# Carried transposes of a head pair, held back in the next pair's list of steps

## The chip, the cores and the metric

The kernel runs on one core of a Trainium2 chip. The metric is device microseconds (us) of one execution; less is better. The engines are called PE (TensorE), DVE (VectorE), ACT (ScalarE), POOL (GpSimd) and SP (SyncE, which issues most loads).

## The reference, cut to what matters

One inference step of a two-layer encoder trunk, in float32, over 1024 new frames of one stream (prompt) and 16 frames of each of 8 running streams (sample, with caches of 1024 past positions). Width 1024, heads of 64, MLP of 4096.

```python
# layer 0: 8 heads of stick-breaking attention beside a convolution branch
z = einsum('bqhd,bkhd->bhqk', q, k) * HEAD_DIM ** -0.5
log_keep = where(k_pos < q_pos, log_sigmoid(-z), 0)
between = cumsum(log_keep, axis=3, reverse=True) - log_keep
w = where(k_pos < q_pos, exp(log_sigmoid(z) + between), 0)
a_out = einsum('bhqk,bkhd->bqhd', w, v)
c_out = silu(layernorm(depthwise_conv31(a * sigmoid(g))))
x = x + concatenate([a_out, c_out]) @ w_out
# layer 1: 16 heads of softmax attention in a band of 9 chunks of 64
s = einsum('bqhd,bkhd->bhqk', q, k) * HEAD_DIM ** -0.5 + rel_bias
p = softmax(where(band, s, -inf))
x = x + (p @ v) @ w_out
# each layer: RMSNorm ahead of the mixer and of a squared-ReLU MLP, residuals; RMSNorm at the end
```

The outputs are the frames of prompt and sample, and the new caches.

## The kernel before

**Tiles and stages.** All 1152 frames are processed together, 128 on the partitions of a tile. A float32 matmul is done as three products of a hi and a lo part (`split`, L185 and L186: ACT copies the hi part, DVE subtracts to the lo part). Projections run in groups of 12 matmuls of 128x384: 8 chunks of 128 inputs by three products are 24, in two steps of 12. The order of the stages is mixer 0, MLP 0, mixer 1, MLP 1, last norm.

**Pairs.** Attention goes by pairs of heads: four pairs p in layer 0, eight in layer 1. A pair has eight jobs (2 heads i by 4 blocks t of 256 queries). A job is: scores for its two sub-blocks of 128 queries (`one`: matmuls `z` at L924 and L925 in layer 0, `zc` at L1201 and L1202 in layer 1), element-wise work on DVE and ACT, transposes of the weights through PE (`turn`: tiles `tpa` from L388 in layer 0, `tpc` from L455 in layer 1), their copies out of PSUM by ACT and DVE (`wa`; `whc` and `wlc`), and products with the values (`prod`: `ava` L398, `avc` L467, joined on DVE in `cpa`, `cpc`). In layer 0 the element-wise work is two ACT activations (`sg`, `kp`), a scan over `kp` on DVE (L907) and a product on DVE (L909), which leaves the weights in `sg`. In layer 1 it is a fused bias and maximum on DVE (L1165), an exponential on ACT (L1168), and a reciprocal and a scale on DVE (L1169, L1170), which leaves the weights in `s`. Names carry pair, head and block: `sg017` is pair 0, head 1, sub-block 7; `tpa0130` is pair 0, head 1, block t=3, group 0.

**What runs beside a pair.** The sample attention of the pair (`zs`, `zn`: scores against cached keys, which are loaded as tiles `ct..k`), the projection of the next pair (`proj`, PSUM tiles `psp` in layer 0 and `psc` in layer 1; in layer 0 also `ag`), and in layer 0 the 31 taps of the depthwise convolution on DVE (L735). In pair 3 of layer 0 the place of the projection is taken by the output projection `psoa`, whose input `cat` is loaded back from HBM (`cr`, L1062) and split.

**What sets the order.** All instructions of an engine run in the order in which the program records them, and that order comes from lists of `Step`s: a step has an estimated PE time `pe` (ns), a function that records its instructions, and, if wanted, a name, the name of a step that it comes `after`, and a `lag` in ns after that step's end. `merge` (L53) interleaves lists: it keeps a model clock `now`, and takes among the heads of all lists the one that is ready first, and among equal ones that whose list is least far along. A list is never reordered in itself, so a head that is not ready holds back all of its list. The first transposes of a job have `after` = the name of the job's last scores, with a lag of 4500 ns (L421, L491).

**Carried steps.** The last job of a pair (head 1, block 3) is not finished in the pair's own list: its transposes and products are `carry`, the first steps of the next pair's list (L985, L1238). There the name they come after is not among the names of the call: `merge` finds no end for it.

```python
steps = carry + [jobs[0][0]] + [Step(327.0, lambda p=p, g=g: expand_v(p, g)) for g in range(NG)]
...
run(level(merge(steps, sample, fill, mix), now))
```

Of the kernel before, what the change touches and what calls it, by code (L numbers as in the profile page):

```python
# [52 lines left out]
def merge(*lists):  # L53


    lists = [steps for steps in lists if steps]
    total = [sum(s.pe for s in steps) or 1.0 for steps in lists]
    at, done = [0] * len(lists), [0.0] * len(lists)
    out, now = [], 0.0
    ends = {s.name: 1e9 for steps in lists for s in steps if s.name}  # L60
    while True:
        heads = []
        for n, steps in enumerate(lists):
            if at[n] < len(steps):
                s = steps[at[n]]
                ready = max(now, ends.get(s.after, -1e9) + s.lag)
                heads.append((ready, (done[n] + 0.5 * s.pe) / total[n], n, s))
        if not heads:
            return out
        now, _, n, s = min(heads, key=lambda e: e[:3])  # L70
        out.append(s)
        at[n] += 1
        done[n] += s.pe
        now += s.pe
        if s.name:
            ends[s.name] = now
# [48 lines left out]
def tile_trunk(ctx, tc, ins, outs):  # L125
# [529 lines left out]
    def mixer0():  # L655
        with ExitStack() as st:
# [309 lines left out]
            for p in range(4):  # L966
# [29 lines left out]
                load = sample_caches(0, p, cp)  # L996
                sample = two_samples(*(sample_steps(0, p, bg, S, wk, load, soft, cs) for bg in range(2)))
                run(level(merge(steps, sample, fill, mix), now))
            return cat_t

# [96 lines left out]
    def mixer1(nx, win):  # L1097
        h, rstd = nx.h, nx.r
        with ExitStack() as st:
# [129 lines left out]
            for p in range(8):  # L1229
# [10 lines left out]
                if p == 7:  # L1240
                    bias_p(p, 0)
                    expand_qk(p)
                    run(merge(steps, ready_chunks(1, range(3), pp, cat_t)))
                    steps = []
# [13 lines left out]
                if p < 7:  # L1258
                    bias_p(p, 0)
                    if p:  # L1260
                        expand_qk(p)
                run(merge(steps, sample, fill, back))
            return cat_t

# [702 lines left out]
```

## Time and profile before

| What | Value |
|---|---|
| Median of 3 runs | 2751.92 us (2749.0 to 2752.41) |
| The profiled execution | 2750.03 us, its span 2748.2 us |
[...]
| PE busy | 2669.0 us (97%) |
| DVE busy | 2090.5 us (76%) |
| ACT busy | 1389.0 us (51%) |
| POOL busy | 328.3 us (12%) |

How to read it: the profile is of one execution, and its own time differs from the median by 1.9 us. The shares are means over stages with different limits. A row of a timeline gives the start and the length of one instruction, or of several alike in a row (x and their count), and in square brackets how long the engine was idle before it and what ended that. A row of windows gives a stretch and, for each engine, its busy time in it with the count of instructions.

### The profile page before, as it was taken

The page shows a single profiled execution, that of the slowest core. Times are in us where ns is not written, and L with a number is a line of the kernel's source. Part 1 is how long each engine was busy: PE and PEld are TensorE (multiplying, and loading weights), DVE is VectorE, ACT ScalarE, POOL GpSimd, SP SyncE. Part 2 cuts the span into 40 slices and gives each one's busy share as a digit, 9 for nine tenths or more (in the row PEclk, how much of TensorE's full clock was granted, in tenths as well). Part 3 has the DMA queues.
Part 4 walks back from the last instruction along what each step waited for, and adds up shares of the span by engine and source line. Part 5 has one row for each costly group of instructions (what it writes and reads, how often), then busy time and mean ns, then how long its engine had stood idle before and what let it go on. Part 6 is the DMA issues. An engine that isn't in the chain of part 4 may idle for free.

```text
span 2748.2 us, 50583 instructions
## 1 busy us (share of the span) xinstructions
PE 2669.0 (97%) x19362; PEld 2557.1 (93%) x19362; DVE 2090.5 (76%) x4117; ACT 1389.0 (51%) x2906; POOL 328.3 (12%) x599
## 2 busy tenths in 40 slices
PE   8999898999999999999999999998999999999998
PEld 8987776799999999999999999997999999999998
DVE  8999998888777755758577777778787777647577
ACT  5344456755554543435355555556555555434344
POOL 1100101041111100000011111110221111100001
PEclk9999999999999999999999999999999999999999
DMA  4434446454343377435444444446533343684344
GB/s 157 121 111 147 118 141 223 145 176 143 139 146 141 138 260 250 124 100 170 146 140 138 140 135 135 139 132 229 179 132 137 141 145 138 230 270 134 96 125 145
DMA packets 173203, 422.90 MB, mean 154 GB/s; under 512 B 25968, under 2 KB 53808, under 8 KB 170912
## 3 DMA queue, kind: packets, MB, share of 16 engines
q1 hardware_dynamic: 135696, 288.38, 33.1%
q0 software_dynamic: 37120, 131.27, 13.9%
q8 instruction: 152, 2.49, 0.4%
q14 instruction: 91, 0.75, 0.1%
q10 hardware_dynamic: 144, 0.02, 0.0%
HBM read 289.60 MB, written 117.34 MB: 148 GB/s over the span
## 4 chain that ended last, share of the span: by engine, by line
PE 76%; DVE 12%; ACT 4%; issue 4%; DMA 3%; POOL 0%; SPq 0%; DVEq 0%; ACTq 0%; POOLq 0%
PE um L1461 25%; PE pd L1686 25%; PE psc L225 10%; PE psp L225 3%; DVE y L735 3%; PE avc L467 2%; PE tpc L455 2%; DVE kp L907 2%; PE f L225 1%; PE psoa L225 1%; DMA cr<-cat_d 1%; PE zc L1201 1%; PE zc L1202 1%; PE zs L568 1%; PE so L602 1%
## 5 line engine op out<-in xcount | busy, mean ns | idle before, releaser
L225 PE MATMUL psc<-h,hl_wc 128*128 128x384 f32 x1728 | 327.2, 339 | 0.0
L225 PEld LDWEIGHTS psc<-h,hl_wc 128*128 128x128 f32 x1728 | 296.8, 188 | 13.3 <-issue 10.9
L1461 PE MATMUL um<-sl,hl_m 128*128 128x288 f32 x1548 | 240.3, 295 | 0.0
L1461 PEld LDWEIGHTS um<-sl,hl_m 128*128 128x128 f32 x1548 | 217.7, 188 | 0.0
L1686 PE MATMUL pd<-tm,hl_wd 128*128 128x288 f32 x1584 | 214.7, 294 | 0.0
L1686 PEld LDWEIGHTS pd<-tm,hl_wd 128*128 128x128 f32 x1584 | 211.3, 189 | 0.0
L735 DVE SCALAR_TENSOR_TENSOR y<-u,dw,y 128x1024 f32<-128x1024 f32 (+1 forms) x232 | 177.8, 806 | 0.6
L225 PE MATMUL psp<-h,hl_wi 128*128 128x384 f32 x864 | 165.7, 344 | 0.0
L1468 ACT ACTIVATE hdm<-hdm 128x288 f32<-128x288 f32 x192 | 84.7, 442 | 156.5 <-DVE hdm L1467 154.8
L225 PEld LDWEIGHTS psp<-h,hl_wi 128*128 128x128 f32 x864 | 150.9, 191 | 7.0 <-issue 6.2
L186 DVE TENSOR_TENSOR tm<-xr,tm 128x576 fp32r<-128x576 f32 (+1 forms) x120 | 85.8, 715 | 93.9 <-ACT tm L185 93.6
L185 ACT ACTIVATE tm<-xr 128x576 fp32r<-128x576 f32 (+1 forms) x120 | 77.6, 646 | 95.8 <-PE pd L1686 74.0
L1168 ACT ACTIVATE s<-s,mxc 128x640 f32<-128x640 f32 (+4 forms) x128 | 88.9, 694 | 60.2 <-DVE mxc L1165 58.6
L1461 PE MATMUL um<-sl,hl 128*128 128x288 f32 x756 | 119.1, 296 | 0.0
L1686 PE MATMUL pd<-th,hl_wd 128*128 128x288 f32 x792 | 113.7, 297 | 3.8 <-DVE th L186 3.7
L1686 PEld LDWEIGHTS pd<-th,hl_wd 128*128 128x128 f32 x792 | 108.2, 190 | 4.8 <-DVE th L186 4.2
L1686 PE MATMUL pd<-xr,hl_wd 128*128 128x288 f32 x792 | 112.4, 296 | 0.0
L1686 PEld LDWEIGHTS pd<-xr,hl_wd 128*128 128x128 f32 x792 | 108.0, 190 | 0.0
L1461 PEld LDWEIGHTS um<-sl,hl 128*128 128x128 f32 x756 | 106.4, 188 | 0.8
L1686 PE MATMUL pd<-tm,hl 128*128 128x288 f32 x768 | 104.9, 295 | 0.0
L1686 PEld LDWEIGHTS pd<-tm,hl 128*128 128x128 f32 x768 | 103.1, 188 | 0.0
L185 ACT ACTIVATE whc<-tpc 128x512 fp32r<-128x512 f32 (+1 forms) x144 | 72.5, 523 | 46.7 <-PE tpc L455 45.8
(526 smaller groups left out, 6637.0 us busy)
## 6 DMA issues: line engine op xcount, KB each, us to landing
xr<-hb_d SPq DMA_DIRECT2D x208, 288.0 KB, 3.0
xr<-in_w_up_dram SPq DMA_DIRECT2D x64, 512.0 KB, 4.2
hb_d<-hdm POOLq DMA_DIRECT2D x96, 288.0 KB, 2.4
hb_d<-t POOLq DMA_DIRECT2D x96, 288.0 KB, 2.4
wm<-in_w_down_dram SPq DMA_DIRECT2D x64, 256.0 KB, 4.0
st_wd<-in_w_down_dram SPq DMA_DIRECT2D x64, 256.0 KB, 3.5
st_wc<-in_w_in_c_dram SPq DMA_DIRECT2D x44, 256.0 KB, 2.9
xm_d<-xo POOLq DMA_DIRECT2D x16, 576.0 KB, 3.5
```

The lines of the kernel that those rows point to most:

```text
L185: ACT(hi, src, AF.Copy)
L186: return tt(lo, src, f(hi), ALU.subtract)
L225: mm(ps()[:, :G], hl[:, a, at:at + P], act[g][k // 4][b][:, k % 4, :], start=n == 0, stop=n == len(todo) - 1)
L455: nc.tensor.transpose(tp[:, c0 + q * P:c0 + (q + 1) * P], blocks.get(j, tile_q), ident)
L467: mm(st["av"][:, o0:o0 + n], vs[:, j, i].rearrange("p a d -> p (a d)"), src[:, c0:c0 + n], start=st["done"] == 0, stop=st["done"] == nmm - 1)
L568: mm(box["z"][at // 512][own, at % 512:at % 512 + kw], qb[:, own], k[:, b * kw:b * kw + kw], start=True, stop=True)
L735: stt(src if j == CW - 1 else dst, src, wj, dst, ALU.mult, ALU.add)
L907: nc.vector.tensor_tensor_scan(keep[:, 0:n][:, ::-1], keep[:, 0:n][:, ::-1], ones[:, 0:1].to_broadcast([P, n]), 1.0, ALU.mult, ALU.mult)
L1168: ACT(s[:, :n], s[:, :n], AF.Exp, bias=mx, scale=-1.0, accum_out=tot)
L1461: mm(banks[b, n][:, :TQ], w[:, a, c * P:c * P + P], combo(key, c)[:, h, n * TQ:n * TQ + TQ], start=k < 3 and c == 0 and i == 0, stop=c == ...
L1468: ACT(y, y, AF.Relu)
L1686: mm(ps, w[:, a, m * P:m * P + P], b[:, h, (n - ns[0]) * TQ:(n - ns[0]) * TQ + TQ], start=first and s == 0, stop=j == NJ - 1 and s == 2, s ...
```

## The change

In `merge`, a head whose `after` names a step that is not in this call had been ready at once (its end taken as minus 1e9 ns). Now the end of such a step is taken as 2000 ns before the start of the list, so that a carried `turn` step with its lag of 4500 ns is ready at 2500 ns of the model clock. Steps without an `after` are treated as before. A blank line is added above, so that every line number behind it is one higher in the changed kernel.

```diff
             if at[n] < len(steps):
                 s = steps[at[n]]
-                ready = max(now, ends.get(s.after, -1e9) + s.lag)
+
+                ready = max(now, ends.get(s.after, -2000.0 if s.after else -1e9) + s.lag)
                 heads.append((ready, (done[n] + 0.5 * s.pe) / total[n], n, s))
```

The order of all five engines differs from boundary 0 to 1 of layer 0 up to that layer's last pair, and from boundary 0 to 1 of layer 1 up to 5 to 6; the last pair of layer 1 and the MLPs stand as before. No instruction is added or left out.

PE at boundary 0 to 1 of layer 0, before (`psp200` is the first projection group of pair 2; `h0` its inputs, `hl_wi` its weights):

```order
L398 MATMUL ava012_2221<-wa0122_2179,vs0_747 64x128
L388 MATMUL tpa0130_2261<-ident_69,sg016_2058 128x128
L225 MATMUL psp200_2268<-h0_00_159,hl_wi12_0_2037 128x384
...
L225 MATMUL psp200_2268<-h0_11_164,hl_wi12_0_2037 128x384
L388 MATMUL tpa0130_2261<-ident_69,sg017_2125 128x128
...
L225 MATMUL psp200_2268<-h0_30_171,hl_wi12_0_2037 128x384
L388 MATMUL tpa0131_2284<-ident_69,sg016_2058 128x128
...
L568 MATMUL zs0100_2298<-ct01k00_2300,qb0_124 32x256 x4
```

and with the change:

```order
L399 MATMUL ava012_2221<-wa0122_2179,vs0_747 64x128
L226 MATMUL psp200_2261<-h0_00_159,hl_wi12_0_2037 128x384
...
L226 MATMUL psp200_2261<-h0_70_190,hl_wi12_1_2042 128x384
L389 MATMUL tpa0130_2291<-ident_69,sg016_2058 128x128
L389 MATMUL tpa0130_2291<-ident_69,sg017_2125 128x128
...
L569 MATMUL zs0100_2307<-ct01k00_2309,qb0_124 32x256 x4
```

Before, five matmuls of the group stand between the first transpose and the first that reads `sg017`; now all 24 stand ahead of both.

PE at the tail of pair 1 of layer 1, before (`zc116` are the scores of sub-block 6, `tpc1120` and `tpc1121` transpose `s114` and `s115`, `sq111` is a transpose of the sample part):

```order
L467 MATMUL avc111_16154<-wlc1111_16122,vs1_14196 128x128
L1202 MATMUL zc116384_16172<-l1_14195,q1_14191 128x256
L225 MATMUL psc222_16141<-h1_40_13712,hl_wc8_1_15619 128x384
...
L225 MATMUL psc222_16141<-h1_70_13826,hl_wc8_1_15619 128x384
L455 MATMUL tpc1120_16195<-ident_69,s114_16093 128x128
L455 MATMUL tpc1120_16195<-ident_69,s115_16125 128x128
...
L610 MATMUL sq111_16213<-ident_69,sb111_16081 128x128
L467 MATMUL avc112_16220<-whc1120_16200,vs1_14196 128x256 x2
```

and with the change:

```order
L1203 MATMUL zc115384_16143<-l1_14195,q1_14191 128x256
L226 MATMUL psc222_16084<-h1_40_13712,hl_wc8_1_15619 128x384
...
L226 MATMUL psc222_16084<-h1_70_13826,hl_wc8_1_15619 128x384
L468 MATMUL avc111_16166<-whc1110_16127,vs1_14196 128x256 x2
...
L1203 MATMUL zc116384_16184<-l1_14195,q1_14191 128x256
L611 MATMUL sq111_16195<-ident_69,sb111_16081 128x128
L456 MATMUL tpc1120_16202<-ident_69,s114_16107 128x128
...
L456 MATMUL tpc1120_16202<-ident_69,s115_16139 128x128
L456 MATMUL tpc1121_16211<-ident_69,s115_16139 128x128
```

The second half of `psc222`, which stood directly ahead of the transposes, now stands one place earlier, ahead of the products `avc111`. Ahead of these, between `zc115` and `avc111`, the first half of `psc222` stood before.

DVE at the same place, before (`sv12` takes `psc222` out of PSUM, `hl_wc10` is a weight split):

```order
L1170 TENSOR_SCALAR s114_16093<-s114_16093,totc114_16104 128x640
L186 TENSOR_TENSOR hl_wc10_0_16288<-st_wc10_0_16286,hl_wc10_0_16288 128x512
L1169 RECIPROCAL totc115_16136<-totc115_16136 128x1
L1165 ISA s116_16168,mxc1160_16175<-zc1160_16169,bp11_15729 128x384
L1170 TENSOR_SCALAR s115_16125<-s115_16125,totc115_16136 128x640
L477 TENSOR_TENSOR cpc111_16165<-avc111_16154,atc111_16163 64x256
```

and with the change:

```order
L1171 TENSOR_SCALAR s114_16107<-s114_16107,totc114_16118 128x640
L1123 TENSOR_TENSOR sv12_15999<-psc222_16084,rh1_14160 128x384
L187 TENSOR_TENSOR hl_wc10_1_16293<-st_wc10_1_16291,hl_wc10_1_16293 128x512
L1170 RECIPROCAL totc115_16150<-totc115_16150 128x1
L478 TENSOR_TENSOR cpc111_16177<-avc111_16166,atc111_16175 64x256
L1171 TENSOR_SCALAR s115_16139<-s115_16139,totc115_16150 128x640
L1166 ISA s116_16180,mxc1160_16187<-zc1160_16181,bp11_15755 128x384
```

Ahead of the scale of `s115` (L1170, now L1171) stand now `sv12` and `cpc111`, and behind it the score step of `s116`.

PE at boundary 2 to 3 of layer 0, before (`psoa` is the output projection, `sg216` and `sg217` are the carried weights):

```order
L398 MATMUL ava212_4408<-wa2122_4381,vs0_747 64x128
L388 MATMUL tpa2130_4460<-ident_69,sg216_4299 128x128
...
L388 MATMUL tpa2131_4487<-ident_69,sg217_4344 128x128
L225 MATMUL psoa000_4494<-cat0_00_4452,hl_wo0a0_0_4479 128x384
L388 MATMUL tpa2132_4501<-ident_69,sg216_4299 128x128
```

and with the change:

```order
L399 MATMUL ava212_4408<-wa2122_4387,vs0_747 64x128
L226 MATMUL psoa000_4480<-cat0_00_4452,hl_wo0a0_0_4472 128x384
L226 MATMUL psoa001_4487<-cat0_00_4452,hl_wo0a0_0_4472 128x384
L389 MATMUL tpa2130_4494<-ident_69,sg216_4339 128x128
L389 MATMUL tpa2130_4494<-ident_69,sg217_4368 128x128
```

Eight transposes stood ahead of the first `psoa`; now two `psoa` stand ahead of them.

## Rows read from the trace of the kernel before

**Rows 1.** Windows: stretch, its length, busy us of each engine, PE clock, DMA.

```profile
106.00:218.00 112.00, 105.00 (x781) 91.27 (x779) 109.64 (x144) 54.35 (x126) 11.04 (x19) 0.99 0.45 133
...
333.00:433.00 100.00, 86.31 (x675) 70.51 (x671) 96.87 (x124) 52.01 (x124) 13.23 (x25) 0.97 0.48 150
...
1580.00:1650.00 70.00, 68.44 (x506) 64.45 (x505) 51.63 (x146) 37.88 (x89) 8.98 (x21) 1.00 0.46 138
```

**Rows 2.** Timeline of PE at boundaries 0 to 1 and 1 to 2, layer 0.

```profile
206.02 4.44 PE L225 MATMUL psp<-h,hl_wi 128*128 128x384 f32 x24
...
219.31 0.90 PE L388 MATMUL tpa<-ident,sg 128*128 128x128 f32 x3 [6.17 <-DVE sg L909]
...
336.51 0.98 PE L388 MATMUL tpa<-ident,sg 128*128 128x128 f32 x7 [2.76 <-DVE sg L909]
```

**Rows 3.** Timeline of DVE at and behind boundary 0 to 1.

```profile
218.03 1.23 DVE L909 TENSOR_TENSOR sg<-sg,kp 128x1023 f32<-128x1023 f32 x1
...
234.48 0.42 DVE L410 TENSOR_TENSOR cpa<-ava,ata 64x256 f32<-64x256 f32 x1 [1.63 <-ACT ata L406]
...
283.33 2.56 DVE L907 TENSOR_TENSOR_SCAN kps<-kps,ones 128x1152 f32<-128x1152 f32 x1 [1.98 <-ACT kps L956]
```

**Rows 4.** Sample scores of pair 2: PE timeline, then landing times of their key loads.

```profile
339.97 0.64 PE L568 MATMUL zs<-ct02k,qb 128*32 128x256 f32 x8
...
349.48 0.64 PE L568 MATMUL zs<-ct02k,qb 128*32 128x256 f32 x8
...
DMA to landing us min/median/max: 3.5/5.9/7.0
```

**Rows 5.** Timeline of PE at boundary 2 to 3, layer 0.

```profile
429.67 1.03 PE L388 MATMUL tpa<-ident,sg 128*128 128x128 f32 x6 [4.14 <-DVE sg L909]
433.27 0.69 PE L225 MATMUL psoa<-cat,hl_wo0a 128*128 128x384 f32 x1 [2.57 <-ACT cat L185]
...
438.33 2.85 PE L1021 MATMUL mu<-yl,ones 128*128 128x384 f32 x8
441.94 2.44 PE L225 MATMUL psoa<-cat,hl_wo0a 128*128 128x384 f32 x12 [0.76 <-ACT cat L185]
```

**Rows 6.** Timeline of PE, tail of pair 1 and boundary 1 to 2, layer 1.

```profile
1500.05 2.27 PE L225 MATMUL psc<-h,hl_wc 128*128 128x384 f32 x12
...
1503.68 2.24 PE L225 MATMUL psc<-h,hl_wc 128*128 128x384 f32 x12
1505.76 1.03 PE L455 MATMUL tpc<-ident,s 128*128 128x128 f32 x8
...
1508.05 0.51 PE L467 MATMUL avc<-whc,vs 128*128 128x256 f32 x2 [1.14 <-ACT whc L185]
...
1514.05 0.88 PE L455 MATMUL tpc<-ident,s 128*128 128x128 f32 x6 [0.36 <-DVE s L1170]
```

**Rows 7.** Timeline of DVE at the same tail.

```profile
1503.91 0.54 DVE L1165 CUSTOM_DVE_ANT_0 s<-zc,bp 128x384 f32<-128x384 f32 x1
...
1504.38 0.55 DVE L1170 TENSOR_SCALAR s<-s,totc 128x640 f32<-128x640 f32 x1
1504.96 0.42 DVE L477 TENSOR_TENSOR cpc<-avc,atc 64x256 f32<-64x256 f32 x1
...
1505.96 0.56 DVE L1122 TENSOR_TENSOR sv<-psc,rh 128x384 f32<-128x384 f32 x1
```

**Rows 8.** Timeline of ACT at the same tail.

```profile
1507.40 1.09 ACT L185 ACTIVATE whc<-tpc 128x512 fp32r<-128x512 f32 x2
```

**Rows 9.** PE waits in the two MLPs, and windows behind them with PE's clock.

```profile
974.85 0.40 PE L1686 MATMUL pd<-th,hl_wd 128*128 128x288 f32 x1 [1.90 <-DVE th L186]
...
2376.89 2.46 PE L1686 MATMUL pd<-th,hl_wd 128*128 128x288 f32 x14 [1.79 <-DVE th L186]
...
975.00:980.00 5.00, 4.92 (x24) 4.69 (x25) 4.96 (x10) 2.05 (x5) 0.20 (x1) 0.66 0.93 307
...
2377.00:2381.00 4.00, 3.93 (x28) 3.70 (x29) 3.97 (x8) 1.81 (x4) 0.46 (x1) 1.00 0.86 275
```

## Prediction

> **What bounds the kernel now.** I read the share of each engine by stretch first, then the waits of TensorE (PE) at the pair boundaries, then what VectorE (DVE) did during them. The windows [rows 1] give two regimes. In layer 0 DVE is busy 109.64 of 112 us before the first boundary and 96.87 of 100 behind the second, and PE 105.00 and 86.31: there DVE sets the pace, and an idle PE costs only what it makes DVE wait for later. In a pair of layer 1 PE is busy 68.44 of 70 us and DVE 51.63: there each wait of PE goes to the end. So one and the same edit has to be priced by two rules.
>
> At boundary 0 to 1 the reader is to see [rows 2] that PE stands 6.17 us for the scaled scores sg; at 1 to 2 it stands 2.76. On DVE the same sg [rows 3] ends at 219.26, behind a queue without a gap. In layer 1 [rows 6] the boundary's wait is only 0.36 us (1514.05); the tail of the pair before it has 1.14 us (1508.05), for the hi part of the transposed weights.
>
> **The change part by part.** In the next pair's list the first carried step is now ready at 2.5 us instead of at once. No instruction is added or removed on any engine; all is order, so every term is a wait.
>
> *A, boundary 0 to 1.* All 24 matmuls of the projection group now stand ahead of the carried transposes, where 5 stood. They last 4.44/24 = 0.185 us each [rows 2], so the 19 more are 3.5 us: PE reaches the transposes about 3.5 us later and waits some 2.7 us instead of 6.17. The transposes themselves start when they did, at 219.3, because DVE's queue up to sg is unchanged. Behind them PE is 3.5 us ahead, so the products are too, and DVE's idle 1.63 us at 234.48 [rows 3], which came from them through ScalarE (ACT), goes. After that DVE is full again. On the queues, a key load goes one place back on SP, but its zs comes some 9 us after its buffer is free, and such loads land in 7.0 at most [rows 4]; POOL, which writes the products out, is busy 11.04 of 112 us [rows 1], so their later place costs nothing. I take -1.6 us. Bounds: 0, if DVE finds the gap elsewhere; -3.6, if the 1.98 us at 283.33 [rows 3] also goes; I stay near the first gap, since the second waits for sample scores whose matmuls are tied to DVE again by then.
>
> *B, boundary 1 to 2.* 24 matmuls, 4.4 us, cover the 2.76 us wait wholly. DVE has 3.1 us idle in the whole stretch behind it [rows 1], none of it in a piece that this boundary makes. Against it, the four sample score groups zs now stand closer: the fourth uses the buffer that the first frees. Before, the first ended at 340.5 and the fourth began at 349.48, 8.9 us apart; now some 4.0 us of work lie between (seven transposes, two zs, twelve matmuls of 2.2 us). Its key load takes 3.5 to 7.0 us, median 5.9 [rows 4], so a new PE wait of about 2 us arises. DVE needs these scores some four taps earlier in its queue, but they also come earlier than at 349.48, so I take 0. Bounds: -0.6 (a part of that pair's DVE idle) and +2.5 (load at its longest, DVE held by it).
>
> *C, boundary 2 to 3.* PE's list now has two output-projection matmuls, which wait for a load, ahead of the transposes that ran in 429.67 to 430.70 [rows 5]. Those 1.03 us move behind 433.27. From there PE ran without a gap to 441.18 and waited 0.76 us at 441.94 for the next load's split [rows 5], so 1.03 - 0.76 = 0.3 us are left. Bounds: 0 (the later waits for loads take it up) and +1.6 (all of it, and again at the lower clock).
>
> *D, six tails and boundaries of layer 1.* The boundary's 0.36 us goes, since 24 matmuls stand there too. But the interleaving of the whole pair shifts by one group of twelve, and at its tail this group no longer stands between the scores of block 5 and the transposes that need them. Before: scores done at 1500.05, transposes at 1505.76, 5.7 us later, of which the group was 2.08 (from 1503.68 [rows 6]) and which one small transpose now replaces by 0.13 (an eighth of the eight in 1.03); so PE is there 3.8 us after the scores. The scale on DVE ended at 1504.93 [rows 7], 4.9 us after them. In DVE's new order the evacuation sv (0.56) and the product cpc (0.42) go ahead of that scale and one score step (0.54) behind it: +0.44, so 5.3. New wait: 5.3 - 3.8 = 1.5 us. In exchange the 1.14 us shrink. ACT began the hi part whc at 1507.40 [rows 8], 1.6 us after the first transpose, because an exponential and a weight split stood ahead; both now stand elsewhere, and what remains is the copy itself (0.55), some 0.2 of hand-over (0.1 each way, as from its end at 1507.95 to the product at 1508.05), less the 0.3 us of two or three more transposes that PE does meanwhile: 0.45. Net per pair: 1.5 - (1.14 - 0.45) - 0.36 = +0.45, six times +2.7 us. Bounds per pair: -0.4 (whc wait gone, new wait only 4.9 - 3.8 = 1.1) and +0.95 (new wait 2.0, if cpc has to wait for ACT); that is -2.4 to +5.7 us.
>
> **Sum.** -1.6 + 0 + 0.3 + 2.7 = +1.4 us against the profiled execution's own 2750.03, so 2751.4; the median of the three runs shown is 1.9 us above that execution, which makes 2753.3 for the median now. All lower ends give -6.6, all upper ends +9.8.
>
> **The rivals.** *One: the waits of layer 0 come back whole.* If DVE's order bends with PE (the taps slide into its gaps), 3.5 us at the first boundary and 2.76 at the second are kept, and layer 1 gives nothing: 6.3 us less, 0.3 for C back, -6.0, so about 2746. For it: the 6.17 us is the longest PE wait of all the pairs. Against it: DVE's 2.4 us of idle in 112 [rows 1]; it cannot go below its own work.
>
> *Two, on the slow side: the new tail wait drops PE's clock.* [...] A stretch like the one at 975 loses 0.34 x 5 = 1.7 us; in all six pairs 10.2 us, which with the sum gives 2763.5; in half of them 2758.4. [...]
>
> *Three: nothing of it is felt.* If the scan on DVE, not the order, sets both sides (the transposes start at 219.3 in any case) and the tails balance, the time stays at 2751.9. This lies inside the forecast's range.
>
> **Chances and range.** 0.2% of the time, 5.5 us, is about what a measurement can tell from no change. The forecast with rival three, 2747 to 2757.5, gets 0.52; rival one 0.22, most of it faster by a little over 0.2%; rival two 0.18; the rest, 0.08, is the load of B or a tail at its upper bound, +6 to +10 us. So faster 0.22, same 0.52, slower 0.26. The range takes rival one and all but the last part of rival two: 2745 to 2762.
>
> **What would show it.** In the profile after: the wait at boundary 0 to 1 near 2.7 us, and that at 1 to 2 gone, with DVE busy no less than before in these windows; a wait of about 2 us for the load at the fourth zs of pair 2; no wait at layer 1's boundaries, but one of 1 to 2 us for the scale at each of six tails, and the one for whc under 0.6. I am wrong if layer 0 is shorter by more than 4 us (then DVE was not the bound), if the tails have no new wait (then D's sign turns), or if half-clock stretches appear in the pairs of layer 1 (then rival two).

## The result and the profile after

| | Median | Range | Runs |
|---|---|---|---|
| before | 2752.41 us | 2747.34 to 2756.27 | 13 |
| with the change | 2759.98 us | 2754.93 to 2766.64 | 13 |

The ratio is 1.0028 with a 95% interval of 1.0021 to 1.0035: slower by 7.6 us, more than the 0.2% that can be told from no change. The time lies in the forecast range, but not where its likeliest case put it. The profiled execution took 2763.35 us, 3.4 above the median, its span 2761.5.

First the windows of the kernel after, the counterparts of [rows 1]: stretch, length, busy time of each engine, PE's clock, DMA.

```profile
106.00:218.00 112.00, 107.97 (x797) 94.23 (x796) 109.61 (x145) 54.15 (x126) 11.04 (x19) 1.00 0.44 134
...
333.00:433.00 100.00, 87.45 (x672) 72.26 (x673) 96.23 (x127) 53.26 (x125) 13.93 (x25) 0.93 0.50 153
...
1580.00:1650.00 70.00, 67.99 (x494) 64.42 (x493) 49.94 (x139) 37.33 (x87) 8.93 (x21) 0.98 0.45 137
```

DVE is as full as before in layer 0 (busy 109.61 of 112 us and 96.23 of 100). In layer 1 PE does fewer instructions in the same 70 us (494 against 506), and its clock is 0.98, no longer 1.00.

PE's waits in layer 0 (timeline; the counterparts of [rows 2, 4, 5]):

```profile
218.94 1.75 PE L389 MATMUL tpa<-ident,sg 128*128 128x128 f32 x7 [2.82 <-DVE sg L910]
...
279.22 0.33 PE L925 MATMUL z<-k,q 128*128 128x128 f32 x1 [1.07 <-DVE u L716]
...
344.88 1.08 PE L569 MATMUL zs<-ct02k,qb 128*32 128x256 f32 x8 [3.40 <-DMA ct02k<-in_sb_k_dram]
...
428.94 1.10 PE L226 MATMUL psoa<-cat,hl_wo0a 128*128 128x384 f32 x2 [5.28 <-ACT cat L186]
...
452.95 3.68 PE L226 MATMUL psoa<-cat,hl_wo0a 128*128 128x384 f32 x9 [2.12 <-ACT cat L186]
459.05 1.65 PE L286 MATMUL rr_l<-sq_l,ones 128*128 128x384 f32 x2 [2.42 <-DVE sq_l L282]
```

The wait at boundary 0 to 1 is 2.82 us instead of 6.17, and that at 1 to 2 is gone. A wait of 3.40 us for the key load has come, and one of 2.42 us for the statistics of the convolution's norm (`rr_l`), which the kernel before does not have.

PE at two tails of layer 1 (the counterparts of [rows 6]), and the windows at these places:

```profile
1510.42 0.87 PE L456 MATMUL tpc<-ident,s 128*128 128x128 f32 x6 [1.59 <-DVE s L1171]
1511.72 0.50 PE L468 MATMUL avc<-whc,vs 128*128 128x256 f32 x2 [0.42 <-ACT whc L186]
...
1582.19 0.87 PE L456 MATMUL tpc<-ident,s 128*128 128x128 f32 x6 [1.59 <-DVE s L1171]
1583.48 0.57 PE L468 MATMUL avc<-whc,vs 128*128 128x256 f32 x2 [0.42 <-ACT whc L186]
```

```profile
1511.00:1517.00 6.00, 5.58 (x28) 5.34 (x27) 5.28 (x15) 5.20 (x9) 1.17 (x3) 0.72 0.61 202
1582.00:1588.00 6.00, 5.39 (x26) 5.16 (x27) 5.23 (x16) 4.90 (x9) 1.50 (x3) 0.72 0.59 186
1654.00:1660.00 6.00, 5.58 (x27) 5.34 (x28) 5.15 (x15) 5.05 (x9) 1.28 (x3) 0.72 0.58 172
```

At the tail stand the two waits that were worked out, and behind them the granted clock is 0.72 of full over 6 us, where [rows 1] have 1.00 in a pair. In windows of 0.5 us behind the first of these tails it is 1.00 up to 1512.0, 0.60 in the next and 0.50 from 1512.5 to 1515.5, and from 1516.0 on 1.00 again. The pairs follow each other every 71.77 us (1510.42 to 1582.19) instead of 70.11. DVE shows why the scale is late (its timeline at the second tail):

```profile
1579.41 0.55 DVE L1171 TENSOR_SCALAR s<-s,totc 128x640 f32<-128x640 f32 x1
1579.88 0.55 DVE L1123 TENSOR_TENSOR sv<-psc,rh 128x384 f32<-128x384 f32 x1
1580.35 0.68 DVE L187 TENSOR_TENSOR hl_wc<-st_wc,hl_wc 128x512 fp32r<-128x512 f32 x1
1580.94 0.15 DVE L1170 RECIPROCAL totc<-totc 128x1 f32<-128x1 f32 x1
1581.13 0.42 DVE L478 TENSOR_TENSOR cpc<-avc,atc 64x256 f32<-64x256 f32 x1
1581.58 0.55 DVE L1171 TENSOR_SCALAR s<-s,totc 128x640 f32<-128x640 f32 x1
```

Between the two scales stand `sv`, the split and `cpc`; the second ends at 1582.13, and PE starts at 1582.19.

### The profile page after: what moved, and what is told of

The parts are those of the page before. It is cut to its first block, busy times and chain, and to the rows that moved or that the text cites. A ratio compares the mean times of both kernels' runs of the same rounds, so it can differ in the third digit from the quotient of the medians.

```text
span 2761.5 us, 50586 instructions
## 1 busy us (share of the span) xinstructions
PE 2682.9 (97%) x19362; PEld 2572.6 (93%) x19362; DVE 2089.5 (76%) x4117; ACT 1392.2 (50%) x2906; POOL 329.1 (12%) x599
## 4 chain that ended last, share of the span: by engine, by line
PE 76%; DVE 13%; issue 5%; DMA 3%; ACT 3%; POOL 0%; SPq 0%; DVEq 0%; ACTq 0%; POOLq 0%
PE pd L1687 25%; PE um L1462 25%; PE psc L226 11%; DVE y L736 3%; PE avc L468 2%; PE psoa L226 2%; PE psp L226 2%; PE tpc L456 2%; DVE kp L908 1%; PE f L226 1%; PE zc L1202 1%; PE zc L1203 1%; PE zs L569 1%; PE so L603 1%; DVE sg L910 1%
```

## The experiments

**The theories.** W+C: the time is lost at the six tails of layer 1, by waits that grow 0.5 us and by a drop of PE's clock behind them; layer 0 about evens out. Rival F: the tails cost their 0.5 us only, and the rest is lost in layer 0. All variants give `merge` a parameter, and the calls that hold pass it:

```diff
-def merge(*lists):
+def merge(*lists, hold=-1e9):
...
-                ready = max(now, ends.get(s.after, -1e9) + s.lag)
+                ready = max(now, ends.get(s.after, hold if s.after else -1e9) + s.lag)
```

| Run | Held at | Median, before's median | Ratio, 95% interval |
|---|---|---|---|
| e1 | layer 0 | 2752.97, 2749.35 | 1.0010, 1.0001 to 1.0019 |
| e2 | layer 1 | 2761.89, 2749.35 | 1.0043, 1.0030 to 1.0055 |
| e3 | 0 to 1 of layer 0 | 2750.06, 2749.35 | 1.0004, 0.9995 to 1.0013 |
| e4 | 2 to 3 of layer 0 | 2757.47, 2749.35 | 1.0029, 1.0019 to 1.0039 |
| e5 | layer 1, steps of 8 | 2760.21 (one run), 2754.06 | none |
| e6 | layer 1, steps of 6 | 2748.52, 2754.06 | 0.9974, 0.9964 to 0.9984 |
| e7 | 2 to 3, statistics later | 2754.91, 2754.06 | 0.9997, 0.9988 to 1.0005 |
| e8 | nowhere, steps of 6 | 2758.44, 2754.06 | 1.0014, 1.0002 to 1.0026 |
| e9 | 1 to 2 of layer 0 | 2750.65, 2751.74 | 0.9995, 0.9986 to 1.0004 |
| e10 | all: the change itself | 2759.85, 2751.74 | 1.0028, 1.0019 to 1.0036 |
| e11 | all, both amendments | 2740.86, 2751.74 | 0.9956, 0.9944 to 0.9969 |
| e12 | 0 to 1 and layer 1, steps of 6 | 2744.33, 2751.74 | 0.9970, 0.9957 to 0.9982 |

Each version is compared with runs of the kernel before on the same chip; e1 to e4, e5 to e8 and e9 to e12 had a chip each, which is why three medians of before stand in the table. The ratio is not quite the quotient of the two medians (e7: 0.9997, where the medians give 1.0003), so differences of that size settle nothing. A second measure comes from the traces: layer 1 from the matmul of its norm's row statistics (`rr_h`, 1338.16 before) to the late transposes of its last pair (1865.14 before).

| Layer 1 | Length |
|---|---|
| not held (before, e1, e3, e4, e7, e9) | 526.94 to 527.03 us |
| held (after, e10, e2) | 535.06, 534.56, 533.89 us |
| held, steps of 6 (e6, e11, e12) | 520.77, 520.72, 520.73 us |
| not held, steps of 6 (e8) | 530.72 us |

Layer 0, from the boundary's transposes (219.31 before) to the matmul of the MLP that waits for `hl_m` on DVE (610.90 before), repeats far worse: the same order took 391.59 (before), 393.90 (e2), 394.55 (e8), 396.18 (e6) and 396.51 us (e5), the last three on one chip. So one trace cannot settle a layer 0 term of a few us; times over several runs can.

**e1 and e2: which layer.** e1:

> The carried transposes are held only at the three boundaries of layer 0; layer 1 has the order of before. Theory W+C (waits and clock): in the profile after the change layer 0 ends 1.5 us later (first matmul of the MLP behind its wait at 612.41 instead of 610.90), so +1 to +3 us, about 2754. Rival F (the loss is all in layer 0 and its clock, the tails of layer 1 cost only their 0.5 us each): +4 to +5 us, about 2757. Either way: wait at boundary 0 to 1 near 2.8 us, a wait of 2 to 4 us for the key load of pair 2, none of it in layer 1, whose pairs keep a period of 70.1 us.

e2:

> Held only at the boundaries of layer 1; layer 0 as before. Theory W+C: each of the six tails has 1.6 and 0.4 us of waits in place of 1.14 and 0.36, and a stretch at half clock behind them, so a period of 71.8 instead of 70.1 us: +8 us, about 2760, which is the whole change. Rival F: the waits alone, +0.5 us six times, +3 us, about 2755, and no stretch at half clock in most pairs.

The calls that hold were these:

```diff
e1
-                run(level(merge(steps, sample, fill, mix), now))
+                run(level(merge(steps, sample, fill, mix, hold=-2000.0), now))
e2
-                run(merge(steps, sample, fill, back))
+                run(merge(steps, sample, fill, back, hold=-2000.0))
```

e1 is +0.10% (2.8 us), as W+C says, with a key load wait of 4.14 us and layer 1 untouched; its interval (0.3 to 5.2 us) alone would also allow F's 4 to 5 us. e2 is +0.43%, at least 0.30%: F's 3 us (0.11%) is refuted. Its trace makes the split within one execution. PE's timeline at its first three tails, windows behind the first two, and windows over the two pairs between the three:

```profile
1507.76 0.87 PE L455 MATMUL tpc<-ident,s 128*128 128x128 f32 x6 [1.59 <-DVE s L1170]
...
1578.38 0.87 PE L455 MATMUL tpc<-ident,s 128*128 128x128 f32 x6 [1.59 <-DVE s L1170]
...
1650.16 0.87 PE L455 MATMUL tpc<-ident,s 128*128 128x128 f32 x6 [1.59 <-DVE s L1170]
```

```profile
1508.00:1514.00 6.00, 5.53 (x37) 4.97 (x35) 5.55 (x18) 5.21 (x9) 1.10 (x2) 1.00 0.69 223
1578.00:1584.00 6.00, 5.20 (x25) 4.96 (x26) 5.51 (x16) 4.90 (x9) 1.64 (x3) 0.72 0.61 206
...
1507.76:1578.38 70.62, 68.53 (x505) 64.64 (x505) 51.65 (x146) 38.48 (x88) 8.93 (x22) 1.00 0.45 136
1578.38:1650.16 71.78, 69.77 (x506) 66.21 (x506) 51.65 (x146) 38.45 (x88) 8.90 (x22) 0.98 0.44 134
```

The wait is the same 1.59 us each time. Behind the first tail the clock stayed at 1.00, and the next pair came after 70.62 us; behind the second it fell, and the next came after 71.78. Against 70.11 before, the waits thus cost 0.51 us per pair and the fall of the clock another 1.16. The 0.51 rests on this one pair, the only one with these waits at full clock. In the pair with the fall PE is busy 1.24 us longer, and its idle time is nearly the same (2.01 against 2.09 us).

**e3, e9 and e4: the three boundaries of layer 0 apart.** The edit is e1's with `hold=-2000.0 if p == 1 else -1e9` (2 and 3 for the others). e3:

> Held only at boundary 0 to 1 of layer 0. Theory: DVE's idle 1.63 us behind this boundary goes and nothing else changes, so PE's waits for u and for sg around 281 and 307 stand 1.6 us earlier, and the time is 1 to 2 us less, about 2750.8. Rival (PE waits come back whole): 3.4 us less or more. Rival (DVE finds the gap elsewhere): no difference at 281.

DVE's gap went, and the wait for `u` (a tile of the convolution branch) came 60.39 us behind the boundary instead of 61.88: 1.5 us gained, as forecast. The time shows none of it (1.0004; the interval ends at 1.4 us of gain). By the trace the lead of 1.5 us still stood at the transposes of boundary 1 to 2 and was down to 0.2 at the next ones (139.69 us behind the boundary against 139.93); between them PE's clock was 0.83 in 330 to 340, where before's was 1.00.

PE at these two places in e3, with DVE's wait between them, and PE in e6, which has before's order here:

```profile
333.60 1.75 PE L388 MATMUL tpa<-ident,sg 128*128 128x128 f32 x7 [2.86 <-DVE sg L909]
...
347.51 0.42 DVE L410 TENSOR_TENSOR cpa<-ava,ata 64x256 f32<-64x256 f32 x1 [1.56 <-ACT ata L406]
...
357.56 0.44 PE L388 MATMUL tpa<-ident,sg 128*128 128x128 f32 x2 [1.75 <-DVE sg L909]
```

```profile
336.26 1.76 PE L388 MATMUL tpa<-ident,sg 128*128 128x128 f32 x7 [2.85 <-DVE sg L909]
...
360.50 0.44 PE L388 MATMUL tpa<-ident,sg 128*128 128x128 f32 x2 [1.75 <-DVE sg L909]
```

The seven transposes took 1.75 us instead of 0.98, and the two places lie 24.0 us apart instead of 22.7. But e2, e5, e6, e7 and e8, which are not held at this boundary, have a fall there too (0.83 to 0.92 in 330 to 340) and 24.2 to 24.3 us; only before and e4 have 22.7. So this trace does not show that the hold lost the lead. The time shows only that no gain of 1.6 us came of it, and why stays open.

e9:

> Held only at boundary 1 to 2 of layer 0. Theory: PE's wait of 2.8 us for sg goes and one of 3 to 4 us for the key load of pair 2 takes its place; from the boundary to 405 the trace loses about 3 us, and then the load of the output projection's input, which the new order of SP's queue issues earlier against the work around it, gives some 4 to 5 us back at 433; in sum -2 to +1 us. Rival (the early projection in the whole change came from two holds together): it stays at 28 us behind the wait of 1.7 us near 405, and the time is +3 us.

```profile
347.56 0.64 PE L568 MATMUL zs<-ct02k,qb 128*32 128x256 f32 x8 [3.81 <-DMA ct02k<-in_sb_k_dram]
...
409.26 0.85 PE L388 MATMUL tpa<-ident,sg 128*128 128x128 f32 x6 [1.68 <-DVE sg L909]
...
432.30 0.69 PE L225 MATMUL psoa<-cat,hl_wo0a 128*128 128x384 f32 x1 [1.47 <-ACT cat L185]
```

SP's timeline shows why the load is late, and PE's what follows its wait:

```profile
340.88 0.34 SPq L192 DMA_DIRECT2D st_wi<-in_w_in_ab_dram  x1
...
342.05 1.48 SPq L537 DMA_DIRECT2D ct02k<-in_sb_k_dram  x3
```

```profile
348.38 3.76 PE L225 MATMUL psp<-h,hl_wi 128*128 128x384 f32 x12
```

In its PE timeline the key load's wait is 3.81 us. The first group of `zs` ended 1.2 us earlier than before (near 339.5), but the key loads were issued at 342.05, 122.6 us behind boundary 0 to 1 against 122.4 before: they stand in SP's queue behind a load of `st_wi`, which waited for DVE's split of `hl_wi`, and that split did not move. Behind the wait the clock was 0.74 in 346 to 352, and twelve matmuls of `psp` took 3.76 us instead of 2.37; DVE's wait of 1.33 us at 352.18 is for them. All five traces held at this boundary have the load's wait (3.23 to 4.14 us) and a lower clock behind it (0.71 to 0.90 in 346 to 352).

The transposes near 409 come 3.7 us later than before, counted from boundary 0 to 1, and the output projection comes 1.1 us earlier: 4.8 us are given back between them. The load of its input was issued 5.8 us ahead of the load behind it in SP's queue instead of 1.25 ahead, and the projection began 6.4 us after that issue instead of 8.5. That the second load had slowed the first was not tried by itself. In sum no difference (0.9995), as the first theory has it.

e4:

> Held only at boundary 2 to 3 of layer 0, where the output projection goes ahead of the carried transposes. In the profile after the change the first output projection started about 5.5 us earlier measured from the point before it, and 6 us were lost again between 453 and 510. If both come from this boundary: the projection near 428 instead of 433.3, a wait for the statistics of the convolution's norm near 459, half clock around it, and in sum -1 to +3 us. If the early start came from boundary 1 to 2: the projection stays near 433 here, and the time is 0 to +1.6 us, my term C.

```profile
432.26 1.10 PE L225 MATMUL psoa<-cat,hl_wo0a 128*128 128x384 f32 x2 [9.23 <-ACT cat L185]
...
455.19 3.75 PE L225 MATMUL psoa<-cat,hl_wo0a 128*128 128x384 f32 x9 [2.06 <-ACT cat L185]
461.37 0.91 PE L285 MATMUL rr_l<-sq_l,ones 128*128 128x384 f32 x2 [2.42 <-DVE sq_l L281]
```

Neither forecast held. The projection starts late (the early start was boundary 1 to 2's), and the wait for the statistics is here too, so the time is 8 us above before's median, 0.29%. In the windows of this run the clock was 0.83 in 450 to 460 and in 460 to 470, and in the same windows before it was 1.00.

**e7: the statistics put back.** To e4's hold comes

```diff
-                     Step(800.0, lambda: box["rows"](), 0.0, None, f"s{name}", 2500)]
+                     Step(800.0, lambda: box["rows"](), 0.0, None, f"s{name}", 4500)]
```

> Held only at boundary 2 to 3 of layer 0, as in the fourth experiment, but the step with the norm's row statistics has a lag of 4500 ns instead of 2500, which puts its matmul behind the output projection's groups again, as before the change. Theory (4.8 of the 6 us that the fourth lost are this matmul's wait of 2.4 us and the half clock behind it): the wait is gone, full clock from 455 to 470, time +1 to +2 us against before, so 5 us under the fourth. Rival (the loss comes from the projection's start, now behind a wait of 9.2 us): no change, +6 to +8 us.

e7's PE timeline, and a window of it:

```profile
435.38 1.10 PE L225 MATMUL psoa<-cat,hl_wo0a 128*128 128x384 f32 x2 [8.76 <-ACT cat L185]
...
465.01 0.81 PE L285 MATMUL rr_l<-sq_l,ones 128*128 128x384 f32 x2
...
458.00:472.00 14.00, 13.62 (x84) 10.82 (x83) 14.00 (x28) 12.08 (x26) 1.10 (x2) 1.00 0.67 210
```

The wait for `rr_l` is gone, the clock is 1.00 from 458 to 472, and the time is that of before (0.9997), though the projection still waits 8.76 us. So what e4 lost came with the matmul of the statistics, which stood ahead of the groups that had covered its wait; how much of it is the wait and how much the clock behind it is not separated. The later statistics without a hold were not tried.

**e5, e6 and e8: the filler at the tail of layer 1.** Layer 1's projection is cut into smaller steps, which leaves a piece of it for the tail:

```diff
 steps += chunk_steps(3 * p + n, got, ahead, h, ks, lambda ps, g, n=n: staged(p, n, ps, g),
-                     f"c{p}{n}")
+                     f"c{p}{n}", per=6)
```

e5 (`per=8`, with e2's hold):

> Held only in layer 1, and its projection runs in steps of 8 matmuls instead of 12, so that a piece of it stands at the tail again: PE has about 4.5 us of work between the scores of block 5 and their transposes instead of 3.8. Scale ready 5.4 us after the scores as in the second experiment: a wait of 0.9 us in place of 1.59. Theory (the clock falls when the tail's waits come to about 2 us together): no stretch at half clock in the pairs and a period near 70.1 us. Rival (any wait at this place drops it): the stretches stay, period 71 us or more.

e6 (with e2's hold):

> Held only in layer 1, projection in steps of 6 matmuls: 5.7 us of work before the tail's transposes and 4.2 at the boundary. Theory (what costs is the missing filler at the tail, not the hold): no wait for the scale at the tails, full clock, period 70.1 us or a little less; time 0 to -3 us against before, and 9 us or more under the second experiment. Rival (the hold itself costs, by what it moves elsewhere): still +5 us or more.

e8 (without it):

> No hold anywhere, only layer 1's projection in steps of 6 matmuls. It tells what of the sixth experiment is the finer steps alone: the wait for whc at the tail (1.14 us) and that at the boundary (0.36; now 3.8 us of work there, so 0.6) should stay near their size, time -2 to +2 us. If the tail's wait goes here too, the hold adds nothing in layer 1.

e5's PE timeline at one tail and at the boundary behind it, and the window there:

```profile
1583.22 0.87 PE L455 MATMUL tpc<-ident,s 128*128 128x128 f32 x6 [0.81 <-DVE s L1170]
1584.51 0.50 PE L467 MATMUL avc<-whc,vs 128*128 128x256 f32 x2 [0.42 <-ACT whc L185]
...
1590.09 1.04 PE L568 MATMUL zs<-ct13k,qb 128*32 128x512 f32 x2
1591.37 0.87 PE L455 MATMUL tpc<-ident,s 128*128 128x128 f32 x6 [0.23 <-DVE s L1170]
1592.17 1.06 PE L568 MATMUL zs<-ct13k,qb 128*32 128x512 f32 x6
```

```profile
1582.00:1588.00 6.00, 4.77 (x34) 4.09 (x33) 5.62 (x19) 4.48 (x9) 1.70 (x4) 1.00 0.57 186
```

The wait is 0.81 us (0.9 was expected), and the clock holds at all five such tails (1.00 in every window of 10 us from 1510 to 1870): the rival, that any wait drops it, falls, as before's 1.14 us at full clock (1.00 in 1508 to 1514) would have told. This does not show that the sum of the waits decides. Its time is a single run and is not used here. The period is 71.27 us (from 1511.95, the tail before), though, and not 70.1: the waits sum to 1.46, as before's did to 1.50, so 1.2 us come from elsewhere. Most of it (1.03 us) is the two rows of `zs`: two of its eight matmuls have been set apart from the other six, and the two pieces take 1.04 and 1.06 us, where all eight together took 1.07 before:

```profile
1587.74 1.07 PE L568 MATMUL zs<-ct13k,qb 128*32 128x512 f32 x8
```

e6 has no wait for the scale at its tails. Two of them in its PE timeline, with the only gap over 0.2 us that a pair has, and a window there:

```profile
1581.42 0.51 PE L467 MATMUL avc<-wlc,vs 128*128 128x256 f32 x2 [0.26 <-DVE wlc L186]
...
1650.54 0.50 PE L467 MATMUL avc<-wlc,vs 128*128 128x256 f32 x2 [0.24 <-DVE wlc L186]
```

```profile
1579.00:1585.00 6.00, 5.71 (x39) 5.02 (x38) 5.50 (x17) 5.02 (x8) 1.64 (x3) 1.00 0.32 115
```

The period is 69.1 us, layer 1 is 6.2 us shorter than before's, and the time 0.26% less: with these steps the hold itself costs nothing. e8's PE timeline at one tail and its boundary:

```profile
1582.35 0.50 PE L467 MATMUL avc<-wlc,vs 128*128 128x256 f32 x2 [0.24 <-DVE wlc L186]
...
1588.35 0.87 PE L455 MATMUL tpc<-ident,s 128*128 128x128 f32 x6 [0.48 <-DVE s L1170]
```

With the same steps and no hold (e8) the tail's wait is 0.24 too, but the boundary has 0.46 to 0.50 us and `zs` is set apart as in e5; its period is 70.9 us and its time 0.14% over before's. So the finer steps mend the tail and the hold mends the boundary; each alone is no gain.

**e10 to e12: the change again, and what can be made of it.** e10:

> The changed kernel itself beside the runs of this call, so that it and the versions below share one chip. By its first measurement +0.21 to +0.35% over before. If the parts add (layer 0 alone +0.10%, layer 1 alone +0.43%): about +0.5%. Tail waits of 1.6 and 0.4 us, periods of 70.6 us where the clock holds and 71.8 where it falls.

The change again measures +0.28%, so its first result stands; in its trace the first five tails have 1.59 and 0.42 us, a clock of 0.72 over the 6 us behind each, and periods of 71.0 to 71.7 us. The parts do not add: e1 and e2 make 0.53% with joint uncertainty of about 0.15. e2's layer 1 is 6.9 us longer (0.25%); what its time has beyond that is not in its trace, which is of the quickest of its runs (2757.64). That stays open.

e11 (all holds, `per=6`, and e7's lag):

> The whole change with two amendments: layer 1's projection in steps of 6 matmuls and the norm's row statistics 4500 ns behind their predecessor. Theory: layer 1 gives -6 to -7 us as in the sixth experiment, layer 0 keeps the key load's wait and loses the wait for the statistics: in sum -5 to -9 us against before. Rival (the sixth experiment's gain needs layer 0's order of before): -2 us or no difference.

e12 (e6 and e3 together):

> Held at boundary 0 to 1 and in layer 1, steps of 6 in layer 1. Theory: as the sixth experiment, with DVE's 1.6 us gap behind boundary 0 to 1 gone besides; since the third experiment gave that back later in layer 0, -6 to -9 us against before.

e11 is the best version: 0.44% under before, 0.7% under the change (2740.86 against 2759.85), and more than the 5 to 9 us that were expected (0.44% are 12). Its layer 1 is as long as e6's (520.72 us), and its layer 0 the shortest of all traces (389.08 us), with the key load's wait (4.11 us) still in it. e12 gains 0.30%, which its layer 1 alone explains (6.3 us, 0.23%, within the interval).

## Why the prediction was right or wrong

**The range held, the likeliest case did not.** 2759.98 lies in 2745 to 2762; but "no change" had 0.52, and the kernel became slower, which had 0.26. What came is rival two, at a chance of 0.18: behind the new wait PE's clock falls, to 0.72 over 6 us at five of the six tails. The sum's own 2753.3 was 6.7 us too low, and the range held only because it had been drawn to take in most of this rival. In the whole change layer 0 about evens out (+0.10% by e1), but not by the terms as they stood: A gained nothing that shows, and C lost.

**A was right in its waits, and its gain does not show in the time.** The wait was forecast at 2.7 us and is 2.82; DVE's gap behind it went, and the next waits stood 1.5 to 1.6 us earlier. What failed is the credit for it: A was put at -1.6 us, and e3's time is 1.0004, with at most 1.4 us gained. "After that DVE is full again" does not hold in e3's trace, where DVE stands 1.56 us for `ata` at 347.51 (0.32 before), behind the transposes at lower clock (0.83 in 330 to 340). Since the same fall comes without the hold (0.83 in e6), it is not shown that this is where the gain went.

**B had its wait, its bound was too narrow.** About 2 us were forecast, 3.23 to 4.14 measured. The work between was sized well (4.2 us in e9, 4.0 forecast), but the load was taken to start when the first group frees its buffer: it started 2.5 us later, behind `st_wi` in SP's queue, and landed some 5.5 us after that. The trace of e9 lost 3.7 us up to 409, more than the upper end of 2.5, for the clock fell behind the wait (0.74 in 346 to 352) and DVE then waited too (1.33 us at 352). That the same order returns 4.8 us at the output projection was not seen at all. The sum, 0, was right (0.9995), by luck: two things that it did not have cancel.

**C was mis-sized.** "0.3 us are left" counted the eight transposes alone. Measured by itself (e4) the boundary costs 0.29%, 8 us, because the matmul of the norm's statistics moved ahead of groups that had covered its wait (e7); I compared the order only next to the boundary. With all three holds layer 0 loses 0.10% (e1), so the other two give a part of it back; that it is the hold at 1 to 2, with its earlier projection, is likely and was not tried apart.

**D was right in its waits.** 1.5 and 0.45 us were forecast at the tail, 1.59 and 0.42 measured; the net +0.45 per pair is +0.51 (70.62 against 70.11). What the sum left out is the clock. In the profile after, five of six tails have a stretch at lower clock (0.72 over 6 us); by e2 each adds 1.16 us. The sixth has a shorter wait (0.87 us) and none (1.00 in 1869 to 1875). 6 x 0.51 + 5 x 1.16 = 8.9 us; the trace has 8.1 for layer 1, and the time 7.6 for the whole kernel.

**Rival two was priced near enough, and its chance was too low.** 1.7 us a stretch were taken from the row at 975, and 0.28 x 6 us at the tail come to the same; 1.16 were measured in e2. The waits behind it did not make up for the rest, as PE's idle time hardly changed (2.09 and 2.01 us): its busy time grew by no more than 1.24 us, and why so little stays open. Two rows of before spoke to it, one each way [rows 9]: behind a wait of 1.90 us the clock was 0.66 over 5 us (0.50 from 976.5 to 979.5), behind one of 1.79 us it stayed at 1.00. The two waits forecast for the tail make 1.95 us, as much as either, and I gave the rival 0.18. The runs have both outcomes as well: 0.72 behind three tails shown above, and 1.00 behind the first tail of e2, after the same waits. Why that one kept the clock stays open.

**The step that none of the terms had.** The list of filler is fixed. Twelve matmuls that are moved to the head of a pair are missing at its tail (layer 1), and groups of the output projection that went early no longer cover the statistics (layer 0). D saw it at one place; as a rule it would have sent me through the whole list.

## What to carry to other kernels

Work that fills a wait comes from a fixed stock: whoever spends more of it at one place should look for the wait that it covered before, down to the end of the list. Smaller steps of filler can serve both ends, as the versions with six matmuls do. Where PE is the bound, price a new wait like the one here (1.59 us, with 0.42 us close behind) with the stretch at lower clock that may follow: it cost 1.16 us where the waits added 0.51.

## What the runs showed of the hardware that was not expected

- The same gaps (1.59 and 0.42 us) left the clock at 1.00 at one tail and lowered it to 0.72 over 6 us at the next, in one execution (e2); with 0.81 and 0.42 us (e5) it stayed at 1.00 at one tail shown and fell at none of the five.
- Eight matmuls on 32-column tiles (`zs`) take 1.07 us together in the kernel before, but 1.04 and 1.06 us when two of them are set apart: the two cost as much as eight.
- Layer 1 repeats within 0.1 us over six kernels of one order, while layer 0 of one order spreads over 4.9 us in five traces.
